# Four buffers for the second layer's weights and stored activations; Hyena's part ahead of the third S5 slice

## The chip, the cores and the metric

The kernel runs on one core of a Trainium2 chip. The metric is the device time of one execution in microseconds (us), the median of several runs. The engines are named as in the profile: PE is TensorE, PEld its weight loads, DVE is VectorE, ACT is ScalarE, POOL is GpSimd, SP is SyncE, which here only issues DMAs. SPq is SP's instruction queue.

## What is computed

One layer of a diffusion backbone for 512 latent tokens of width 1024, with 256 context tokens. First a mixer: half of the projected width goes through an S5 state-space model, the other half through a Hyena operator (gated long convolutions by Fourier transforms). Then PEER, which takes for each token and each of 8 heads the 16 best of 16,384 one-neuron experts:

```python
def block(hb):
    q = (hb @ wq).astype(f32).reshape(hb.shape[0], PEER_HEADS, 2, PEER_DK_HALF)
    ...
    e = (jnp.take_along_axis(i1, ci // PEER_TOPK, axis=-1) * PEER_NKEYS
         + jnp.take_along_axis(i2, ci % PEER_TOPK, axis=-1))
    g = jax.nn.softmax(sc, axis=-1)
    act = jax.nn.gelu(jnp.einsum('chkd,cd->chk', jnp.take(u_tab, e, axis=0), hb).astype(f32))
    return jnp.einsum('chk,chkd->cd', (g * act).astype(hb.dtype), jnp.take(v_tab, e, axis=0))
```

All of it is float32. The tables `u_tab` (the experts' first layer) and `v_tab` (their second layer) hold 16,384 rows of 1024 each, 64 MB a table.

## The kernel before

The program is one stream of instructions that a scheduler orders for each engine before it runs; every engine then works through its own list in order. A tile comes from a pool with a fixed number of buffers (`bufs`); an instruction that writes a tile waits until the readers of the tile that held the buffer before are done.

**The mixer** (up to about 480 us). A loop over eight S5 slices (`s_` from 0 to 7) calls `states` and `from_states`; `added(s_ + 1)` prepares the next slice. Ahead of slice `HYAT` it calls `hyena()`, which projects Hyena's half of the width, runs its transforms and multiplies its half of the output projection (`wout_half(1)`). After the last slice PE transposes the S5 result (`pyt`), and the gated linear unit and `wout_half(0)` follow.

**PEER for the first 128 tokens** takes a gather: `gathered(s)` reads for each of 128 experts places one row of both tables per token with an indirect DMA from POOL into `uvr` (1 MB, three buffers), and DVE makes the dot product (`junk`, L1430) and adds the weighted second half to `accg` (L1438). The 128 gathers are spread over the rest of the program, some 0.6 of one in each pass of the loop below while its index is under 88, 1.5 after that.

**PEER for the other 384 tokens** is dense. `first(i)` multiplies the block of 128 experts `i` of the first layer with the tokens and keeps the activation; 88 blocks (`NRUN`) are made ahead and stored in DRAM as `GA[i]`. The gates come from one-hot products (`gates`, L1558) and are stored in DRAM as `GD`.

**The last loop** (about 1060 to 1820 us) runs over the 128 blocks. Each pass is `second(i, ga)`: SP loads the block's second-layer weights `vr` (L1592, 512 KB), every fourth pass a tile of gates `gc` (L1595, 768 KB), and while `i` is under 88 the stored activation `gal` (L1602, 192 KB). ACT and DVE split `vr` into a high and a low part, `vh` (L1598) and `vl` (L1599); DVE multiplies activation and gate (`gw`, L1604), ACT and DVE split that (`wwh` L1607, `wwl` L1608); PE adds 18 products to six accumulators `pacc`. From pass 87 on `first` makes the remaining 40 blocks between the passes; the scheduler pulls some of these ahead.

The buffers in question are those of `mp`, whose default is two: `vr` has `NVR = 2`, `gal` and `yf` (the residual at the end, L1650) two, `gc` two, `vh`, `vl`, `wwh` and `wwl` three each. SP issues all these loads in one list, in order. So the load of `vr` for pass `i` waits at the head of that list until `vl` of pass `i - 2` is made.

```python
vr = mp.tile([P, D], F32, tag="vr", name=f"vr{i}", bufs=NVR)
nc.sync.dma_start(vr, I["uv"][i * P:(i + 1) * P, D:2 * D])
...
A.activation(vh, vr, AF.Copy)
(V if QUIET or i >= P - VLV else GP).tensor_tensor(vl, vr, vh.bitcast(F32), ALU.subtract)
```

Of the kernel before, what the change touches and what calls it, by code (L numbers as in the profile page):

```python
# [9 lines left out]
F32 = mybir.dt.float32  # L10
F32R = mybir.dt.float32r
# [3 lines left out]
AF = mybir.ActivationFunctionType  # L15
ALU = mybir.AluOpType
AX = mybir.AxisListType

P = 128
D = 1024  # L20
# [65 lines left out]
ND = L - NG  # L86
# [9 lines left out]
GH = 2.0  # L96
NOO = 3
S5M = 1
HYAT = 4
GCN = 4  # L100
FQ = 1
MERGE = 1
RECTS = ((0, 1, 16), (1, 1, 8), (2, 2, 5), (4, 4, 3), (8, 8, 1))
NCAND = 54 if MERGE else 50
NVR = 2
NVH = 3
VLV = 2
AHEAD = 2
# [119 lines left out]
def build(tc, I, out, dbg=None, stop=None):  # L228
# [37 lines left out]
    def ps5(name):  # L266
        return ps.tile([P, 512], F32, tag="p5", name=name, bufs=NP5)
# [4 lines left out]
    def psa(name):  # L272
        return pap.tile([P, 512], F32, tag="pa", name=name)
# [13 lines left out]
    def b2(name, shape, dtype=F32):  # L287
        return cur[0].tile(shape, dtype, tag="b2", name=name, bufs=nb2[0])
# [4 lines left out]
    def sm(name, shape, dtype=F32, bufs=1, tag=None):  # L293
        return cur[0].tile(shape, dtype, tag=tag or name, name=name, bufs=bufs)

    def wblock(src, name, lo_eng=None):
        raw = wp.tile([P, D], F32, tag="wraw", name=name + "r", bufs=NRAW)
        ld(raw, src)
        hi = wp.tile([P, D], F32R, tag="wh", name=name + "h")
        lo = wp.tile([P, D], F32R, tag="wl", name=name + "l")  # L300
        nc.scalar.activation(hi, raw, AF.Copy)
        (lo_eng or (nc.vector if FQ else nc.gpsimd)).tensor_tensor(lo, raw, hi.bitcast(F32), ALU.subtract)
        return hi.rearrange("p (k m) -> p k m", m=P), lo.rearrange("p (k m) -> p k m", m=P)
# [29 lines left out]
    V = nc.vector  # L333
    A = nc.scalar
    GP = nc.gpsimd
    FG = V if FQ else GP
    PE = nc.tensor
# [341 lines left out]
    for part in SEQ.split():  # L679
# [36 lines left out]
        elif part[0] == "S":  # L716
            t0, t1 = ((0, 4), None, (4, 6))[n_]
# [21 lines left out]
        elif part[0] == "P":  # L739
# [5 lines left out]
            if NWARM:  # L745
# [5 lines left out]
                for i in range(NWARM):  # L751
                    mm = PE.matmul(pwarm, warm[:, 0:P], warm, start=True, stop=True)
# [457 lines left out]
    for s_ in range(NSL):  # L1210
        vs = VS
        if s_ + 1 < NSL:
            VS = added(s_ + 1)
        if s_ == HYAT:
            hyena()
# [32 lines left out]
    def g2_(name, shape):  # L1248
        return sg_(name, shape, tag="g2", bufs=NG2)
# [10 lines left out]
    for co in range(4):  # L1260
        wg = sg_(f"wg{co}", [P, 4, P], tag="wg", bufs=2)
        nc.sync.dma_start(wg, I["w_glu"][co].rearrange("p (k m) -> p k m", m=P))
        pg = ps5(f"pg{co}")
# [8 lines left out]
        t = g2_(f"cat5{co}", [P, 512])  # L1272
# [24 lines left out]
    for k in range(8):  # L1297
        t = b2(f"h2t{k}", [P, 512])
# [39 lines left out]
    iotak = sm("iotak", [P, P])  # L1338
# [119 lines left out]
    def gathers(share, after):  # L1458
        due[0] += share
        while due[1] < min(P, due[0]):  # L1460
            gathered(due[1], after)
            due[1] += 1

    for hd in range(8):
# [3 lines left out]
        for e in range(2):  # L1468
            ct = 2 * hd + e
            wh, wl = wblock(I["w_q"][ct], f"wq{ct}", V if FQ or QUIET and ct >= 2 else GP)  # L1470
            pq = psa(f"pq{ct}")
# [23 lines left out]
    def columns(lt, eid, gt):  # L1495

        ei = sm(f"ei{lt}", [P, 2, P], I32, tag="ei", bufs=2)
        V.tensor_copy(ei[:, 0], eid)
        V.tensor_scalar(ei[:, 1], ei[:, 0], 127, None, ALU.bitwise_and)
        V.tensor_scalar(ei[:, 0], ei[:, 0], 7, None, ALU.logical_shift_right)  # L1500
        ef = sm(f"ef{lt}", [P, 2, P], tag="ef", bufs=2)
        V.tensor_copy(ef, ei)
        ptr = ps.tile([P, 512], F32, tag="psc", name=f"ptr{lt}", bufs=2 if RGATE else 3)[:, 0:3 * P].rearrange("p (e n) -> p e n", e=3)
        PE.transpose(ptr[:, 0], ef[:, 0], ident)
        PE.transpose(ptr[:, 1], ef[:, 1], ident)
        PE.transpose(ptr[:, 2], gt, ident)
        if RGATE:
            t = sm(f"cols{lt}", [P, 2, P], tag="cols", bufs=3)
            A.activation(t, ptr[:, 0:2], AF.Copy)
            g = sm(f"colg{lt}", [P, 2, P], F32R, tag="colg", bufs=3)  # L1510
            A.activation(g[:, 0], ptr[:, 2], AF.Copy)
            V.tensor_tensor(g[:, 1], ptr[:, 2], g[:, 0].bitcast(F32), ALU.subtract)
            return t, g.bitcast(F32)
        t = sm(f"cols{lt}", [P, 5, P], tag="cols", bufs=3)
        A.activation(t[:, 0:3], ptr, AF.Copy)
        A.activation(t[:, 3:5], ptr[:, 0:3:2], AF.Copy, scale=-1.0)
        return t

    def gates_r(b_, cols, c0):
        cols, g = cols  # L1520
        st = sm(f"gst{b_}", [P, P, SG], tag="gst", bufs=2)
        for q in range(SG // 4):
            pg = ps.tile([P, 4, 2, P], F32, tag="pgg", name=f"pgg{b_}_{q}", bufs=2)
            t0 = c0 + 4 * q
            oo = sm(f"oo{b_}_{q}", [P, 4, 2, P], F32R, tag="oo", bufs=NOO)
            os_ = sm(f"os{b_}_{q}", [P, 4, 2, P], F32R, tag="os", bufs=NOO)
            V.tensor_tensor(oo, iotak.unsqueeze(1).unsqueeze(1).broadcast_to((P, 4, 2, P)),
                            cols[:, :, t0:t0 + 4].rearrange("p e t -> p t e").unsqueeze(3).broadcast_to((P, 4, 2, P)), ALU.is_equal)
            for e in range(4):
                for h in range(2):  # L1530
                    A.activation(os_[:, e, h], oo[:, e, 0].bitcast(F32), AF.Copy, scale=g[:, h, t0 + e:t0 + e + 1])
            for e in range(4):
                mm = PE.matmul(pg[:, e].rearrange("p h i -> p (h i)"), oo[:, e, 1], os_[:, e].rearrange("p h i -> p (h i)"), start=True, stop=True)
            groups.append(mm)
            so = st[:, :, 4 * q:4 * q + 4]
            A.activation(so, pg[:, :, 0].rearrange("p t i -> p i t"), AF.Copy)
            last = V.tensor_tensor(so, pg[:, :, 1].rearrange("p t i -> p i t"), so, ALU.add)
            gathers(G_SHARE, last)
            run_ahead(RG)
        nc.scalar.dma_start(GD[b_], st)  # L1540
# [32 lines left out]
    cols = [columns(lt, eids[:, lt], gts[:, lt]) for lt in range(1, 4)]  # L1573
# [8 lines left out]
    mp = ms.enter_context(tc.tile_pool(name="mp", bufs=2))  # L1582
# [6 lines left out]
    def second(i, ga):  # L1589
        nonlocal gc  # L1590
        vr = mp.tile([P, D], F32, tag="vr", name=f"vr{i}", bufs=NVR)
        nc.sync.dma_start(vr, I["uv"][i * P:(i + 1) * P, D:2 * D])  # L1592
        if i % GCN == 0:
            gc = mp.tile([P, ND // SG, GCN, SG], F32, tag="gc", name=f"gc{i}")
            nc.sync.dma_start(gc, GD[:, :, i:i + GCN, :].rearrange("b p i t -> p b i t"))  # L1595
        vh = mp.tile([P, D], F32R, tag="vh", name=f"vh{i}", bufs=NVH)
        vl = mp.tile([P, D], F32R, tag="vl", name=f"vl{i}", bufs=NVH)
        A.activation(vh, vr, AF.Copy)  # L1598
        (V if QUIET or i >= P - VLV else GP).tensor_tensor(vl, vr, vh.bitcast(F32), ALU.subtract)  # L1599
        if ga is None:  # L1600
            ga = mp.tile([P, ND], F32, tag="gal", name=f"gal{i}")
            nc.sync.dma_start(ga, GA[i])  # L1602
        gw = mp.tile([P, ND], F32, tag="gw", name=f"gw{i}")
        V.tensor_tensor(gw.rearrange("p (b t) -> p b t", t=SG), ga.rearrange("p (b t) -> p b t", t=SG), gc[:, :, i % GCN], ALU.mult)  # L1604
        wh = mp.tile([P, ND], F32R, tag="wwh", name=f"wwh{i}", bufs=NVH)
        wl = mp.tile([P, ND], F32R, tag="wwl", name=f"wwl{i}", bufs=NVH)
        A.activation(wh, gw, AF.Copy)  # L1607
        last = V.tensor_tensor(wl, gw, wh.bitcast(F32), ALU.subtract)  # L1608
        held.append((i, wh, wl, vh, vl))
        if i < P - HOLD or i == P - 1:  # L1610
            for t in range(NT):
                ts_ = slice(t * P, (t + 1) * P)
                for e in range(2):
                    es_ = slice(e * 512, (e + 1) * 512)
                    for (n, ah_, al_, bh_, bl_) in held:
                        mm3(pacc[t][e], (ah_[:, ts_], al_[:, ts_]), (bh_[:, es_], bl_[:, es_]), n == 0, n == P - 1)
            held.clear()
        return last
# [25 lines left out]
    def residual(t):  # L1644
        xr = mp.tile([P, D], F32, tag="xf", name=f"xf{t}", bufs=4)
        nc.sync.dma_start(xr, X1R[t * P:(t + 1) * P])
        y = mp.tile([P, D], F32, tag="yf", name=f"yf{t}")
        ssq = mp.tile([P, 4], F32, tag="ssq", name=f"ssq{t}", bufs=4)
        for e in range(2):
            V.tensor_tensor(y[:, hs[e]], accg[:, hs[e]] if t == 0 else pacc[t - 1][e], gx2[:, hs[e]], ALU.mult)  # L1650
            (GP if t in T_ADD else V).tensor_tensor(xr[:, hs[e]], y[:, hs[e]], xr[:, hs[e]], ALU.add)
            A.activation(junk[:, hs[e]], xr[:, hs[e]], AF.Square, accum_out=ssq[:, e:e + 1])
        ends.append((xr, ssq))
# [44 lines left out]
```

## Time and profile before

| | |
|---|---|
| Time, median of 3 runs | 1841.48 us (1838.68 to 1842.52) |
| The profiled execution | 1842.49 us |
| Its span, first to last instruction | 1840.7 us |
| Busy: PE, DVE, ACT, POOL | 1692.0, 1492.1, 821.4, 157.6 us |
| Mean granted clock of TensorE | 0.968 |

The page cuts the span into 40 slices of 46 us; a digit is the busy share in tenths. The DMA line is the mean busy share of the core's 16 DMA engines, the line under it what they moved. Windows give the same as numbers for any stretch. Lists of waits say which engine sat idle, for whom, how long in total and how often. Matmuls are pipelined: the busy time of PE counts each with its whole length, while the next one starts earlier, so the distance between starts is the price of one.

### The profile page before, as it was taken

How to read it: one execution, taken by the hardware profiler on the slowest of the kernel's cores; microseconds unless marked ns; L12 is line 12 of the kernel's file. 1: busy time of each engine (PE TensorE's matmuls, PEld its weight loads, DVE VectorE, ACT ScalarE, POOL GpSimd, SP SyncE). 2: the span in 40 equal slices, each digit the busy share in tenths (PEclk: the TensorE clock that was granted, in tenths of full speed). 3: DMA queues.
4: the chain of work that ended last, by engine and by line, in shares of the span. 5: the costliest groups of instructions: out<-in, count | busy, mean ns of one | idle time of the engine just before them, and what ended most of it. 6: DMA issues, size and time to landing. Idle time of an engine off the chain costs nothing.

```text
span 1840.7 us, 24953 instructions
## 1 busy us (share of the span) xinstructions
PE 1692.0 (92%) x8729; PEld 1420.7 (77%) x8731; DVE 1492.1 (81%) x3039; ACT 821.4 (45%) x1616; POOL 157.6 (9%) x158
## 2 busy tenths in 40 slices
PE   5799998879999999999999898989898898999997
PEld 2477654447799999989999886767676777999996
DVE  8866999967689988899999766777787777888886
ACT  3444453134533332348988633343333343444444
POOL 0000000000000000001101101111111112121211
PEclk9899998989899999999999998999999999999998
DMA  9436452322444444466898998999989888999981
GB/s 373 146 99 205 160 173 53 75 71 84 126 151 148 146 148 135 145 233 251 325 335 320 341 350 296 311 331 315 331 311 336 302 279 328 360 329 341 342 312 58
DMA packets 170228, 436.13 MB, mean 237 GB/s; under 512 B 17139, under 2 KB 102004, under 8 KB 150902
## 3 DMA queue, kind: packets, MB, share of 16 engines
q1 hardware_dynamic: 128854, 251.28, 40.6%
q0 software_dynamic: 18432, 134.23, 20.2%
q10 hardware_dynamic: 22816, 49.03, 7.3%
q8 instruction: 69, 1.13, 0.2%
q14 instruction: 57, 0.47, 0.1%
HBM read 381.52 MB, written 52.92 MB: 236 GB/s over the span
## 4 chain that ended last, share of the span: by engine, by line
PE 47%; DVE 13%; DMA 13%; ACT 2%; issue 2%; DVEq 0%; ACTq 0%; SPq 0%
DMA vr<-in_uv_dram 11%; PE pa L308 7%; PE pa L306 6%; PE pa L307 6%; PE pacc L307 5%; PE pacc L306 5%; PE pgg L1558 5%; PE pacc L308 5%; DVE vl L1599 2%; PE pq L308 2%; PE pq L306 2%; PE pq L307 2%; ACT vh L1598 2%; DVE idx L1351 1%; DVE rs L1349 1%
## 5 line engine op out<-in xcount | busy, mean ns | idle before, releaser
L307 PE MATMUL pacc<-vl,wwh 128*128 128x512 f32 x768 | 305.8, 399 | 4.7 <-DVE vl L1599 4.7
L308 PE MATMUL pacc<-vh,wwl 128*128 128x512 f32 x768 | 298.0, 397 | 0.0
L306 PE MATMUL pacc<-vh,wwh 128*128 128x512 f32 x768 | 237.1, 402 | 42.8 <-ACT vh L1598 42.7
L1429 POOL DMA_INDIRECT uvr<-in_uv_dram,gidx x128 | 145.2, 1134 | 1148.1 <-DVE accg L1438 810.5
L1599 DVE TENSOR_TENSOR vl<-vr,vh 128x1024 fp32r<-128x1024 f32 x128 | 156.1, 1222 | 94.8 <-ACT vh L1598 94.6
L306 PEld LDWEIGHTS pacc<-vh,wwh 128*128 128x128 f32 x768 | 144.7, 192 | 83.2 <-ACT vh L1598 55.2
L1598 ACT ACTIVATE vh<-vr 128x1024 fp32r<-128x1024 f32 x128 | 135.0, 1057 | 162.3 <-DMA vr<-in_uv_dram 126.5
L307 PEld LDWEIGHTS pacc<-vl,wwh 128*128 128x128 f32 x768 | 148.0, 193 | 38.1 <-DVE vl L1599 7.4
L308 PEld LDWEIGHTS pacc<-vh,wwl 128*128 128x128 f32 x768 | 147.6, 192 | 31.1
L1438 DVE SCALAR_TENSOR_TENSOR accg<-uvr,wgt,accg 128x1024 f32<-128x1024 f32 x128 | 163.7, 1279 | 4.0 <-ACT wgt L1435 1.2
L1430 DVE SCALAR_TENSOR_TENSOR junk<-uvr,hrow 128x1024 f32<-128x1024 f32 x128 | 155.9, 1218 | 2.2 <-DMA uvr<-in_uv_dram,gidx 2.2
L1607 ACT ACTIVATE wwh<-gw 128x384 fp32r<-128x384 f32 x128 | 66.5, 520 | 131.7 <-PE pacc L307 92.3
L1558 PE MATMUL pgg<-o,o 128*128 128x128 f32 x768 | 95.3, 278 | 4.3 <-ACT o L1554 4.3
L1558 PEld LDWEIGHTS pgg<-o,o 128*128 128x128 f32 x768 | 94.3, 195 | 4.5 <-ACT o L1554 4.5
L1608 DVE TENSOR_TENSOR wwl<-gw,wwh 128x384 fp32r<-128x384 f32 x128 | 70.8, 553 | 32.8 <-ACT wwh L1607 32.7
L1549 DVE TENSOR_TENSOR o<-iotak,cols 128x512 f32<-128x512 f32 x96 | 65.9, 686 | 10.3 <-PE pgg L1558 10.3
L1556 DVE TENSOR_SCALAR o<-iotak,cols 128x128 f32<-128x128 f32 x240 | 70.2, 343 | 0.0
L1433 ACT ACTIVATE wgt<-dots 128x1 f32<-128x1 f32 x128 | 25.4, 199 | 87.4 <-DVE junk L1430 87.1
L1554 ACT ACTIVATE o<-o,cols 128x128 f32<-128x128 f32 x144 | 63.6, 493 | 0.2
L1368 ACT ACTIVATE ga<-pa 128x384 f32<-128x384 f32 x128 | 60.4, 472 | 2.7 <-PE pa L308 2.7
L1560 ACT ACTIVATE gst<-pgg 128x512 f32<-128x512 f32 x96 | 56.7, 591 | 2.5 <-PE pgg L1558 2.2
L1604 DVE TENSOR_TENSOR gw<-gal,gc 128x384 f32<-128x384 f32 x88 | 48.4, 553 | 9.1 <-DMA gal<-GA 8.6
(1812 smaller groups left out, 4141.4 us busy)
## 6 DMA issues: line engine op xcount, KB each, us to landing
vr<-in_uv_dram SPq DMA_DIRECT2D x128, 512.0 KB
GD<-gst ACTq DMA_DIRECT2D x12, 2048.0 KB
gc<-GD SPq DMA_DIRECT2D x32, 768.0 KB
GA<-ga ACTq DMA_DIRECT2D x88, 192.0 KB
gal<-GA SPq DMA_DIRECT2D x88, 192.0 KB
wb<-in_w_ada_dram SPq DMA_DIRECT2D x32, 512.0 KB
wa<-in_w_ada_dram SPq DMA_DIRECT2D x8, 1024.0 KB
KD<-kk SPq DMA_DIRECT2D x16, 256.0 KB
```

The costliest lines, as they stand in the source:

```text
L306: nc.tensor.matmul(o, a[0], b[0], start=start, stop=False)
L307: nc.tensor.matmul(o, a[0], b[1], start=False, stop=False)
L308: nc.tensor.matmul(o, a[1], b[0], start=False, stop=stop_)
L1429: GP.indirect_dma_start(out=uvr, out_offset=None, in_=I["uv"], in_offset=bass.IndirectOffsetOnAxis(ap=gidx[:, s:s + 1], axis=0))
L1430: ins = V.scalar_tensor_tensor(junk, uvr[:, 0:D], 1.0, hrow, ALU.mult, ALU.mult, accum_out=dots[:, s:s + 1])
L1438: V.scalar_tensor_tensor(accg, uvr[:, D:2 * D], wgt[:, s:s + 1], accg, ALU.mult, ALU.add)
L1556: last = V.tensor_scalar(o1[:, e], iotak, cols[:, 0, t:t + 1], cols[:, 2, t:t + 1], ALU.is_equal, ALU.mult)
L1558: mm = PE.matmul(pg[:, e, :], o2[:, e], o1[:, e], start=True, stop=True)
L1598: A.activation(vh, vr, AF.Copy)
L1599: (V if QUIET or i >= P - VLV else GP).tensor_tensor(vl, vr, vh.bitcast(F32), ALU.subtract)
L1607: A.activation(wh, gw, AF.Copy)
L1608: last = V.tensor_tensor(wl, gw, wh.bitcast(F32), ALU.subtract)
```

## The change

`NVR` goes from 2 to 4, so `vr` has four buffers. `gal` gets four as well (`NGAL`). The residual's `yf`, two buffers of its own before, now shares those of `vr`. `HYAT` goes from 4 to 2, so `hyena()` stands ahead of the third slice in the source, and the scheduler orders the mixer anew. The diff also rewrites `gates_r` and its branch of `columns`; `RGATE` is 0 in both kernels, so neither is in the program, and every engine gets the same set of instructions in both.

```diff
-HYAT = 4
+HYAT = 2
 GCN = 4
+NGAL = 4
...
-NVR = 2
+NVR = 4
...
         if ga is None:
-            ga = mp.tile([P, ND], F32, tag="gal", name=f"gal{i}")
+            ga = mp.tile([P, ND], F32, tag="gal", name=f"gal{i}", bufs=NGAL)
             nc.sync.dma_start(ga, GA[i])
...
-        y = mp.tile([P, D], F32, tag="yf", name=f"yf{t}")
+        y = mp.tile([P, D], F32, tag="vr", name=f"yf{t}", bufs=NVR)
```

SP's list in the middle of the last loop, around the tile of gates for passes 52 to 55, before (in `vr44_11615` 44 is the pass, the rest a running number):

```order
L1592 DMA vr44_11615<-in_uv_dram 128x1024
L1592 DMA vr45_11649<-in_uv_dram 128x1024
L1602 DMA gal48_11765<-GA_3935 128x384
L1602 DMA gal49_11803<-GA_3935 128x384
L1595 DMA gc52_11907<-GD_7124 128x12x128
L1592 DMA vr46_11687<-in_uv_dram 128x1024
L1602 DMA gal50_11835<-GA_3935 128x384
L1592 DMA vr47_11725<-in_uv_dram 128x1024
```

The same place after:

```order
L1600 DMA vr47_11725<-in_uv_dram 128x1024
L1610 DMA gal50_11835<-GA_3935 128x384
L1610 DMA gal51_11873<-GA_3935 128x384
L1603 DMA gc52_11907<-GD_7124 128x12x128
L1600 DMA vr48_11757<-in_uv_dram 128x1024
L1610 DMA gal52_11913<-GA_3935 128x384
L1600 DMA vr49_11797<-in_uv_dram 128x1024
L1610 DMA gal53_11945<-GA_3935 128x384
```

Against the same tile of gates the loads of `vr` and `gal` stand two passes earlier.

DVE's list at the end of the mixer, before (H7 to Ci7 and ct belong to the last S5 slice; spt, sp, yy, x2t, catz and rzl to Hyena; YC1 is the S5 result that `pyt` waits for):

```order
L585 TENSOR_TENSOR ru07_3363<-ru07_3363,ru17_3364 128x256 x2
L585 TENSOR_TENSOR Cr7_3372<-ct17_3374,ct27_3375 128x512
L1166 TENSOR_TENSOR sp13_2717<-spt130_2725,spt131_2726 128x512
L1167 TENSOR_TENSOR sp13_2717<-spt132_2727,spt133_2728 128x512
L585 TENSOR_TENSOR ct17_3374<-PC1_871,cre_94 128x512
L585 TENSOR_TENSOR ct27_3375<-PC0_870,cre_94 128x512
L585 TENSOR_TENSOR Ci7_3373<-ct17_3374,ct27_3375 128x512
L1041 TENSOR_TENSOR YC1_1325<-YC1_1325,pk10_3392 128x8x64
```

The same place after:

```order
L586 TENSOR_TENSOR ru07_3363<-ru07_3363,ru17_3364 128x256 x2
L1193 TENSOR_TENSOR yy0_2511<-eo0_2509 128x256
L1194 TENSOR_TENSOR yy0_2511<-eo0_2509 128x256
L586 TENSOR_TENSOR Cr7_3372<-ct17_3374,ct27_3375 128x512
L1195 TENSOR_TENSOR x2t_1674<-x2t_1674,yy0_2511 128x512
L586 TENSOR_TENSOR ct17_3374<-PC1_871,cre_94 128x512
L586 TENSOR_TENSOR ct27_3375<-PC0_870,cre_94 128x512
L1199 TENSOR_SCALAR catz0_2515<-x2t_1674,small_91 128x512
L586 TENSOR_TENSOR Ci7_3373<-ct17_3374,ct27_3375 128x512
L480 TENSOR_TENSOR rzl0_2524<-zsq0_2521,rzh0_2523 128x512
L1042 TENSOR_TENSOR YC1_1325<-YC1_1325,pk10_3392 128x8x64
```

The work on Hyena's first output block now stands between the last steps of the last slice, and the step from `sp13` stands ahead of them.

## Rows read from the trace of the kernel before

**Rows 1.** Page, the span in 40 slices of 46 us: PE, DMA share, GB/s.
```profile
PE   5799998879999999999999898989898898999997
DMA  9436452322444444466898998999989888999981
GB/s 373 146 99 205 160 173 53 75 71 84 126 151 148 146 148 135 145 233 251 325 335 320 341 350 296 311 331 315 331 311 336 302 279 328 360 329 341 342 312 58
```

**Rows 2.** Windows of the last loop: stretch, busy us (instructions) by engine, clock, DMA.
```profile
1062.00:1155.00 93.00, 85.98 (x377) 73.02 (x377) 61.65 (x84) 33.72 (x59) 10.01 (x9) 0.92 0.93 321
1155.00:1504.00 349.00, 314.45 (x1322) 250.27 (x1321) 258.37 (x346) 130.94 (x234) 42.26 (x42) 0.98 0.92 318
1504.00:1560.00 56.00, 50.00 (x223) 42.32 (x222) 46.11 (x58) 22.80 (x45) 14.98 (x11) 0.94 0.86 310
1560.00:1820.00 260.00, 260.00 (x1320) 237.15 (x1319) 209.32 (x262) 115.74 (x220) 47.45 (x41) 1.00 0.86 307
```

**Rows 3.** The same windows, instructions on the accumulators pacc alone (PE, PEld, DVE).
```profile
1062.00:1155.00 93.00, 63.66 (x247) 49.17 (x248) 0.00 (x0) 0.92 0.93 321
1155.00:1504.00 349.00, 312.36 (x1309) 247.88 (x1307) 0.00 (x0) 0.98 0.92 318
1504.00:1560.00 56.00, 39.86 (x158) 30.86 (x156) 0.00 (x0) 0.94 0.86 310
1560.00:1820.00 260.00, 131.95 (x556) 103.97 (x557) 0.00 (x0) 1.00 0.86 307
```

**Rows 4.** Waits of 1155 to 1504: total us, times, longest.
```profile
ACT vh L1598 <- DMA vr<-in_uv_dram: 88.1, 52, 5.5
DVE vl L1599 <- ACT vh L1598: 65.2, 38, 6.4
PE pacc L306 <- ACT vh L1598: 33.2, 24, 4.8
```

**Rows 5.** Waits of SP's own queue, same stretch.
```profile
SPq L1592 <- DVE vl L1599: 115.3, 63, 3.8
SPq L1602 <- DVE gw L1604: 111.0, 54, 4.8
```

**Rows 6.** Chain that ended last, same stretch by line; then pieces: start us, us.
```profile
by line: DMA vr<-in_uv_dram 53.3%; DVE vl L1599 8.2%; ACT vh L1598 7.2%; PE pacc L307 7.1%; PE pacc L306 7.1%; PE pacc L308 6.4%; issue 5.7%; DMA gal<-GA 1.5%; DVE junk L1430 1.5%; DVE gw L1604 1.4%; ACT wwh L1607 0.9%; DVE wwl L1608 0.9%; 
...
1300.89 6.57 DMA vr<-in_uv_dram
...
1307.48 1.07 ACT vh L1598
```

**Rows 7.** DMA from 1062 to 1504: packets; the gathers' queue (share of 16 engines).
```profile
DMA packets 71296, 140.94 MB, mean 319 GB/s; under 512 B 4174, under 2 KB 52302, under 8 KB 64744
...
q0 software_dynamic: 7344, 53.48, 33.0%
```

**Rows 8.** Timeline, first products of two passes that follow without a pause.
```profile
1279.83 1.52 PE L306 MATMUL pacc<-vh,wwh 128*128 128x512 f32 x6
...
1283.91 1.52 PE L306 MATMUL pacc<-vh,wwh 128*128 128x512 f32 x6
```

**Rows 9.** Timeline: the issue of one gather and the first use of its data.
```profile
1282.64 1.01 POOL L1429 DMA_INDIRECT uvr<-in_uv_dram,gidx  x1 [5.93 <-DVE accg L1438]
...
1298.50 1.22 DVE L1430 SCALAR_TENSOR_TENSOR junk<-uvr,hrow 128x1024 f32<-128x1024 f32 x1
```

**Rows 10.** Gathers from 1090 to 1820: issue to landing.
```profile
DMA to landing us min/median/max: 5.5/8.2/11.0
```

**Rows 11.** Windows at the mixer's end, columns as in rows 2.
```profile
322.00:368.00 46.00, 36.94 (x174) 20.34 (x175) 46.00 (x80) 7.49 (x17) 0.10 (x1) 0.93 0.32 75
368.00:414.00 46.00, 32.70 (x156) 22.71 (x155) 30.26 (x49) 18.05 (x33) 0.00 (x0) 0.89 0.23 70
```

**Rows 12.** DVE timeline at the last slice; in brackets idle us before, and for whom.
```profile
377.67 0.69 DVE L1041 TENSOR_TENSOR YC<-YC,pk 128x512 f32<-128x512 f32 x1 [1.47 <-PE pk L1038]
...
400.75 0.69 DVE L1055 TENSOR_TENSOR wout12l<-wout12r,wout12h 128x512 fp32r<-128x512 f32 x1 [0.68 <-ACT wout12h L1054]
```

More of the change, by code (lines that the diff above doesn't have):

```diff
@@ L1507, in columns @@
         if RGATE:
[L1508 to L1513, printed above, removed]
+            t = sm(f"cols{lt}", [P, P], tag="cols", bufs=3)
+            A.activation(t, ptr[:, 1], AF.Copy)
+            gh_ = sm(f"colg{lt}", [P, P], F32R, tag="colg", bufs=3)
+            A.activation(gh_, ptr[:, 2], AF.Copy)
+            V.tensor_tensor(ptr[:, 2], ptr[:, 2], gh_.bitcast(F32), ALU.subtract)
+            return t, gh_.bitcast(F32), ptr
         t = sm(f"cols{lt}", [P, 5, P], tag="cols", bufs=3)
@@ L1519, in gates_r, with per_token @@
     def gates_r(b_, cols, c0):
-        cols, g = cols
+        i2, gh_, ptr = cols
         st = sm(f"gst{b_}", [P, P, SG], tag="gst", bufs=2)
+        def per_token(x, t0):
+            return x[:, t0:t0 + 4].unsqueeze(2).broadcast_to((P, 4, P))
         for q in range(SG // 4):
@@ L1524, in gates_r @@
             t0 = c0 + 4 * q
-            oo = sm(f"oo{b_}_{q}", [P, 4, 2, P], F32R, tag="oo", bufs=NOO)
+            o2 = sm(f"o2_{b_}_{q}", [P, 4, P], F32R, tag="o2", bufs=NOO)
+            o1 = sm(f"o1_{b_}_{q}", [P, 4, P], tag="o1", bufs=NOO)
             os_ = sm(f"os{b_}_{q}", [P, 4, 2, P], F32R, tag="os", bufs=NOO)
-            V.tensor_tensor(oo, iotak.unsqueeze(1).unsqueeze(1).broadcast_to((P, 4, 2, P)),
-                            cols[:, :, t0:t0 + 4].rearrange("p e t -> p t e").unsqueeze(3).broadcast_to((P, 4, 2, P)), ALU.is_equal)
+            keys_ = iotak.unsqueeze(1).broadcast_to((P, 4, P))
+            GP.tensor_tensor(o2, keys_, per_token(i2, t0), ALU.is_equal)
+            V.tensor_tensor(o1, keys_, per_token(ptr[:, 0], t0), ALU.is_equal)
+            V.tensor_tensor(os_[:, :, 1], o1, per_token(ptr[:, 2], t0), ALU.mult)
             for e in range(4):
-                for h in range(2):
-                    A.activation(os_[:, e, h], oo[:, e, 0].bitcast(F32), AF.Copy, scale=g[:, h, t0 + e:t0 + e + 1])
+                A.activation(os_[:, e, 0], o1[:, e], AF.Copy, scale=gh_[:, t0 + e:t0 + e + 1])
             for e in range(4):
-                mm = PE.matmul(pg[:, e].rearrange("p h i -> p (h i)"), oo[:, e, 1], os_[:, e].rearrange("p h i -> p (h i)"), start=True, stop=True)
+                mm = PE.matmul(pg[:, e].rearrange("p h i -> p (h i)"), o2[:, e], os_[:, e].rearrange("p h i -> p (h i)"), start=True, stop=True)
             groups.append(mm)
```

## The prediction

> **What bounds the kernel now.** First the page's slices [rows 1]: from the 20th slice on the DMA engines are nearly always busy, and PE, at 9 tenths before, falls to 8 every other slice or so between the 23rd and the 34th. That is the last loop up to pass 87. The windows give it numbers [rows 2]: from 1560 on PE is busy for 260.00 of 260 us, with the loads of both tables beside it, so this part is bound by PE. From 1155 to 1504 PE has 314.45 of 349 us, DVE 258.37, ACT 130.94, and the DMA engines are 0.92 busy.
>
> Then the waits of that stretch [rows 4]: ACT waits 88.1 us in 52 places for `vr`, DVE 65.2 us for `vh`, and PE for `vh`. One chain, seen at three engines. SP's own queue tells why `vr` is late [rows 5]: it waits 63 times for `vl`, the last reader of the buffer that `vr` goes into. The chain that ended last says it once more: 53.3% of the stretch is `vr` on its way [rows 6]. One turn of it: issued at 1300.89 as soon as `vl` freed the buffer, used at 1307.48, 6.57 us later.
>
> How much room is there? PE's busy time hides it, since products overlap. From one pass's first product to the next one's is 4.08 us when nothing waits [rows 8], for 18 products, 0.227 us each. In 1155 to 1504 stand 1309 products on `pacc` [rows 3], 72.7 passes: 4.80 us a pass. A product of `first` is shorter: in 1560 to 1820 PE is full, so (260 - 556 x 0.227) / 764 = 0.175 us [rows 2, 3].
>
> **The change part by part.** It was profiled at 1842.5 us, 1.0 over the median; I make the sum on the profile and take it from the median.
>
> *Four buffers for* `vr`, from 1062 to 1504 (442 us). SP's list after the change puts the load two passes earlier against the other loads, and the buffer it waits for was freed two passes earlier. So a load has nearly four passes (some 16 us) instead of two, for a transfer that took 6.57 us; the wait on `vl` is gone as a cause. What is late next? Three floors.
>
> PE: 247 + 1309 products on `pacc` at 0.227 and 130 + 13 others at 0.175 [rows 2, 3] make 353 + 25 = 378 us. This would give back 64 us and no more.
>
> DMA by busy share: 0.92 to 0.93 now [rows 2]. The same transfers with the engines never idle take 442 x 0.92 = 407 us: 35 us back.
>
> DMA by bytes: 140.94 MB go through in this stretch [rows 7], and no work is taken out. The fullest slice with gathers and loads together moved 360 GB/s [rows 1], so 392 us: 50 us back. At the 350 GB/s of the 24th slice, where PE stayed at 9 tenths, it is 403 us.
>
> So DMA binds before PE does. I take 404 us (349 GB/s), **38 us back**: near the floor by busy share, since that is measured on just these transfers, and a little better, because where two queues hold packets on one engine the share counts both. For the range: 15 us (share only to 0.95) to 50.
>
> The Trainium skill speaks to this ("DMA: Bandwidth & Descriptors", Specifications): it puts what one core can get from HBM at about 358 GB/s. By that this stretch takes at least 394 us, 48 us back, and the PE floor can't be reached. The trace has the page's first slice at 373 GB/s [rows 1], so it is no hard limit here; but with both queues no slice is above 360, which agrees.
>
> *The first passes after it*, 1504 to 1560: PE is busy 50.00 of 56 us [rows 2]; by count 158 x 0.227 + 65 x 0.175 = 47 us, so up to 9 us are there. The rate of gathers goes from 0.6 to 1.5 a pass here, which deeper buffers don't change: **3 us**, between 0 and 9. From 1560 on PE is full: nothing.
>
> *Four buffers for* `gal`: SP waits 111.0 us in this place [rows 5], but in this stretch no engine is listed as waiting for `gal`. What it does is let SP reach the next `vr` sooner; it is part of the 38 us and nothing by itself.
>
> *`yf` in the buffers of* `vr`: the four last `vr` are read by `vl` before the residual begins, so no new wait: 0.
>
> *`hyena()` ahead of the third slice*: the same instructions in another order. DVE is full to 368 [rows 11], so a change of order gains nothing there. After that it is busy 30.26 of 46 us. Between 376 and 401 it idles nine times, 0.6 to 1.7 us each, for PE and ACT (the first and the last: [rows 12]), some 9 us in all. The new order puts Hyena's first output block among the last steps of the last slice, which fills the first of these pauses, but puts five short operations ahead of `YC1`, which `pyt` waits for. Bounds: 9 us back if all pauses close, 6 lost if two or three more of that length open. I take **2 us back**, since two pauses are filled and a part of it is paid by `YC1`. PE is the bound from here to pass 0, so the difference is not swallowed later.
>
> Sum: 38 + 3 + 2 = 43 us; 1841.5 - 43 = **1798 us**.
>
> **The rivals.**
>
> *DMA is the bound already.* For it: 0.92 busy. Then more loads in flight only wait longer beside each other, and the share creeps to 0.95: 442 x (1 - 0.92 / 0.95) = 14 us, time 1827; with nothing at all back, 1841. Against it: 53.3% of the chain is `vr` alone, with SP standing at `vl` before each load, and the wait of ACT ends some 6 us after the issue, most of which is queue time that could begin earlier.
>
> *It doesn't do what it says: SP's list holds the loads up elsewhere.* `vr48` stands behind `gc52` and `gal51`, each of which waits for a `gw`; if those come free only shortly before `vl`, the load gets three passes and not four. For it: SP already waits 111.0 us for `gw` [rows 5]. Against it: none of these waits is longer than 4.8 us, little over a pass. Half of the 38 us: 1841.5 - 19 - 3 = 1820.
>
> *PE is the bound after all*: 64 + 2 us back, 1775. It needs 140.94 MB in 378 us, 373 GB/s, more than any slice with both queues moved.
>
> *Slower: the gathers starve.* Place: `junk` on DVE, ahead of `vl` in the same list. A gather is issued when its buffer is free and used 15.86 us later [rows 9]; it lands after 8.2 us, at most 11.0 [rows 10], so DVE hardly waits. With shorter passes the lead falls to 15.86 x 404 / 442 = 14.5 us, and SP's queue, always filled, takes more of the engines. 53.48 MB at 1.05 MB [rows 7] are 51 gathers; each us over the lead costs 51 us. From 15.4 us on, the 43 us are gone; at 16 us it is 1841.5 - 43 + 76 = 1875. Against it: landing would have to double.
>
> The Trainium skill has a rule on it ("DMA: Bandwidth & Descriptors", Queues, rings and completion order): an engine goes round robin between the queues that have work. By that a gather keeps half of the engines; half of 360 GB/s moves 1.05 MB in 5.8 us, and the lead holds. No run yet shows it with SP's queue always full; it is why this rival gets so little.
>
> **How the numbers follow.** Forecast 0.62; DMA bound already 0.17; held up elsewhere 0.10; PE bound 0.07; gathers 0.04. The range: low, the DMA floor by bytes with 50 + 9 + 6 = 65 us, 1776; high, 15 us, 1826. It holds the forecast, the delayed case and about half of the first rival: 8 in 10. Within 0.2% (3.7 us, about what a measurement of this kernel can tell from no change) lies the poorest end of the first rival, 0.04; slower is the starved gather and a bad order of the mixer without the gain, 0.04; faster 0.92.
>
> **What would show it.** Right: in the last loop up to pass 87 some 4.4 us a pass; SP's wait for `vl` and ACT's for `vr` down to a fraction of 115.3 and 88.1 us; DMA share near 1 and 345 to 360 GB/s; the part after 1560 as long as before; gathers landing later, but under 14 us. Wrong: the same GB/s with longer loads (first rival); SP standing at `gw` before each `vr` (second); 4.1 us a pass with DMA under 0.95 (third); DVE idle before `junk` (fourth). If the mixer ends more than 9 us earlier or 6 us later, the order counts for more than I give it.

## The result, and the profile after

The changed kernel takes **1781.09 us** (median of 4 runs, 1779.70 to 1784.46); the kernel before, on the same chip, 1841.59 us. The ratio is 0.9677, 95% interval 0.9659 to 0.9695: 60 us gained, where 43 were forecast. The profiled execution took 1782.07 us, its span 1780.3 us.

Where they lie, by landmarks in the two traces (us from the start of the span; the load of `vr` 0 is SP's issue, `vh` 87 and 97 are ACT's copies of these passes):

| | before | after | gained in between |
|---|---|---|---|
| load of `vr` 0 | 1059.9 | 1057.6 | 2.3 |
| `vh` of pass 87 | 1503.3 | 1446.3 | 54.7 |
| `vh` of pass 97 | 1559.2 | 1498.8 | 3.4 |
| last product on `pacc` | 1828.6 | 1768.2 | 0.0 |

So nearly all of it is in the stretch of the first 88 passes. From here on "the stretch" is the time from the load of `vr` 0 to `vh` 87: 443.4 us before, 388.7 after. From pass 14 to 87 a pass takes 4.29 us instead of 4.77.

Windows of the changed kernel, in the order of [rows 2]: the stretch, busy us (instructions) of PE, PEld, DVE, ACT and POOL, granted clock, DMA share, GB/s. The four stretches answer to the four of [rows 2], moved by what was gained ahead of them.

```profile
1059.00:1133.00 74.00, 73.95 (x338) 63.44 (x339) 56.87 (x81) 30.91 (x54) 12.21 (x8) 0.97 1.04 377
1133.00:1447.00 314.00, 303.88 (x1336) 248.76 (x1335) 260.26 (x347) 129.30 (x235) 47.86 (x43) 1.00 1.01 360
1447.00:1499.00 52.00, 52.00 (x247) 45.11 (x246) 43.93 (x56) 21.96 (x44) 11.35 (x9) 1.00 0.91 322
1499.00:1760.00 261.00, 261.00 (x1324) 238.00 (x1323) 213.54 (x268) 117.18 (x224) 54.44 (x43) 1.00 0.86 309
```

PE is full or close to it in all four, the DMA engines are at 1.01 to 1.04 in the first two, and the last row is that of [rows 2] again. The page's slices say the same, beside [rows 1]: from the 25th on PE no longer falls to 8 every other slice, and five slices in a row move 356 to 387 GB/s.

```profile
PE   5799998789899999998999989999999999999997
...
DMA  9436453122444444446989899999999998999981
GB/s 372 155 98 209 156 170 91 51 75 71 124 156 139 141 147 151 145 147 246 330 319 333 322 321 387 385 356 378 363 353 358 357 339 320 342 327 349 335 311 71
```

The waits of the second stretch (total us, times, longest):

```profile
ACT wwh L1615 <- PE pacc L308: 131.1, 70, 4.1
...
PE pacc L307 <- ACT vh L1606: 8.4, 7, 1.3
DVE vl L1607 <- ACT vh L1606: 4.8, 6, 1.2
```

Of [rows 4] the first row is gone: ACT no longer waits for `vr`. DVE's 65.2 us for `vh` are 4.8, PE's 33.2 are 8.4. What ACT waits for most now is PE, to give a buffer of `wwh` back. PE's granted clock was 0.92 and 0.98 in the first two stretches of [rows 2] and is 0.97 and 1.00 now: before, 49 products of these passes started 0.40 to 0.45 us after the one ahead of them, where 0.227 is usual; after the change none did. What these slow products cost before isn't shown, since PE was not the bound then (`l_before` below).

SP's own queue, though, looks as it did [rows 5]:

```profile
SPq L1610 <- DVE gw L1612: 124.9, 54, 4.3
SPq L1600 <- DVE vl L1607: 83.4, 61, 7.4
```

SP still stands at `vl` and `gw` before most loads, since it runs ahead until every buffer is taken. These waits now cost nothing: in passes 14 to 87 a load of `vr` is used 9.2 to 18.4 us after its issue (median 13.1), before 3.5 to 11.1 (median 6.3). The chain of the same stretch, against [rows 6], where `vr` on its way had 53.3%:

```profile
by line: PE pacc L308 29.9%; PE pacc L309 29.1%; PE pacc L307 28.6%; issue 2.6%; DVE junk L1431 1.5%; DMA gal<-GA 1.5%; ACT vh L1606 1.3%; DVE vl L1607 1.2%; ACT wwh L1615 0.9%; PE pa L309 0.7%; PE pa L307 0.7%; PE pa L308 0.7%; DVE gw L161
```

Last the DMA view of both first stretches together, beside [rows 7]: the same 141 MB in 388 us, and the share of the gathers' queue and of SP's (q1) add up to more than 1.

```profile
DMA packets 71373, 140.91 MB, mean 363 GB/s; under 512 B 4174, under 2 KB 52302, under 8 KB 64905
...
q1 hardware_dynamic: 64105, 87.81, 66.0%
q0 software_dynamic: 7244, 52.79, 35.2%
```

### The profile page after: what moved, and what is told of

It reads as the page before. It is cut to its first block, busy times and chain, and to the rows that moved or that the text cites. A ratio compares the mean times of both kernels' runs of the same rounds, so it can differ in the third digit from the quotient of the medians.

```text
span 1780.3 us, 24942 instructions
## 1 busy us (share of the span) xinstructions
PE 1670.0 (94%) x8731; PEld 1410.6 (79%) x8731; DVE 1491.0 (84%) x3039; ACT 817.9 (46%) x1616; POOL 169.5 (10%) x158
## 4 chain that ended last, share of the span: by engine, by line
PE 63%; DVE 12%; issue 1%; ACT 1%; DMA 1%; ACTq 0%; DVEq 0%
PE pacc L308 9%; PE pacc L309 9%; PE pacc L307 9%; PE pa L309 7%; PE pa L307 7%; PE pa L308 7%; PE pgg L1566 5%; PE pq L309 2%; PE pq L307 2%; PE pq L308 2%; DVE idx L1352 1%; DVE rs L1350 1%; PE pg L1266 1%; DVE idx L1348 1%; PE po L307 1%
## 5 line engine op out<-in xcount | busy, mean ns | idle before, releaser
L308 PE MATMUL pacc<-vl,wwh 128*128 128x512 f32 x768 | 299.6, 391 | 1.8 <-DVE vl L1607 1.8
L1430 POOL DMA_INDIRECT uvr<-in_uv_dram,gidx x128 | 157.1, 1228 | 1090.6 <-DVE accg L1439 764.6
L308 PEld LDWEIGHTS pacc<-vl,wwh 128*128 128x128 f32 x768 | 144.1, 188 | 33.6 <-DVE vl L1607 3.6
```

The source lines that it names most:

```text
L308: nc.tensor.matmul(o, a[0], b[1], start=False, stop=False)
L1430: GP.indirect_dma_start(out=uvr, out_offset=None, in_=I["uv"], in_offset=bass.IndirectOffsetOnAxis(ap=gidx[:, s:s + 1], axis=0))
```

## The experiments

Ratios are to the kernel before, measured beside each run, so they can be set beside 0.9677 of the change. Gains in us are differences of medians; by the ratios they come out some 3 us otherwise at most. In the last loop the scheduler ordered the lists of ACT, DVE and SP anew in each of these kernels, so that a few us can also come from the order. Theory 1 was that `vr` had been issued too late for its landing time and that PE is the bound now. The rivals: DMA is the bound now, SP's list or `gal` held the loads up, or the order of the mixer gave more than it seems.

### The parts of the change alone

The buffers without the order (`p_bufs`, against the changed kernel):

```diff
-HYAT = 2
+HYAT = 4
```

> All of the change except HYAT, which stays 4. Theory 1 (late loads of vr were the loss, and the mixer's order gave 2.2 us): the loop as in the changed kernel, pass 0 begins 2 us later, 1783 us. Rival A (the new order of the mixer counts for more than its 2.2 us at pass 0, because the loop's instructions are ordered anew as well): over 1788 us.

Measured: 1786.42 us, ratio 0.9693 (0.9663 to 0.9723). The stretch takes 393.5 us. The buffers make nearly the whole gain; the order's share, 0.0016 or 3 us, is within the intervals.

The order without the buffers (`p_hyat2`, against the kernel before):

```diff
-HYAT = 4
+HYAT = 2
```

> HYAT = 2 alone, all buffers as before. Theory 1: the first transpose of the S5 result and the first pass of the last loop come 1 to 3 us earlier, the passes stay at 4.8 us, 1839 us. Rival A: the loop changes too, under 1834 us.

Measured: 1837.69 us, ratio 0.9959 (0.9939 to 0.9980): 7.6 us gained against the 1845.26 us measured beside it, more than the 1 to 3 of theory 1, and as much as rival A asked for (under 1834 us, with 1841.5 before). Where it is gained is seen only roughly, since the one profiled run took 1832.05 us, 5.6 less than the median. In that run it isn't the mixer: `pq`, the first product after it, starts at 479.3 us (479.5 before). By pass 14 the run is 7.4 us ahead. With another order of the mixer the lists of DVE, ACT and SP differ around the first passes of the loop too, on SP in some ten places, and are the same after that. That this makes the 7.6 us is not shown: from the load of `vr` 0 to `vh` 14 `p_hyat2` takes 87.2 us and the kernel before 94.9, but `l_before` below, with `HYAT` = 4 and fewer products, 87.0 as well.

How far the mixer can be told apart at all shows in two kernels whose lists on PE are the same up to the last loop, `p_gal3` and `p_vr3` below. Their first products of `pq` (duration ns min/median/max, first and last start up to 486 us):

```profile
L307 PE MATMUL pq<-h2h,wq0h x6: 387/395/796, 476.8 to 485.2; 128*128 128x512 f32 x6
```

```profile
L307 PE MATMUL pq<-h2h,wq0h x3: 398/632/768, 481.5 to 485.6; 128*128 128x512 f32 x3
```

The same order starts it at 476.8 and at 481.5 us. Over all profiled runs it starts at 479.9 us on average with `HYAT` = 2 (8 kernels) and at 480.0 with 4 (6 kernels). The 2.3 us of the table above are within this scatter.

Four buffers for `vr` alone (`p_vr4`):

```diff
-HYAT = 2
+HYAT = 4
...
-NGAL = 4
+NGAL = 2
```

> Four buffers for vr alone (yf shares them, as in the change, since the memory does not hold both); gal keeps two, HYAT stays 4. Theory 1: 4.3 us a pass, 1783 us, as with four buffers for gal. Rival B (SP, held at the load of gal until gw frees its buffer, gets to vr only a pass later): half of the gain in the loop, some 1812 us, with ACT waiting again for vr.

Measured: 1813.30 us, ratio 0.9831 (0.9802 to 0.9860), about half of the gain: rival B's number, but not by its mechanism. ACT waits for `gw`, not for `vr`; the waits of 1138 to 1475:

```profile
ACT wwh L1615 <- DVE gw L1612: 60.1, 38, 3.4
...
DVE gw L1612 <- DMA gal<-GA: 34.0, 20, 4.0
```

And its chain there, with one of its longest pieces (start us, us):

```profile
by line: DMA gal<-GA 26.3%; PE pacc L307 17.1%; PE pacc L309 16.6%; PE pacc L308 16.2%; issue 4.0%; ACT vh L1606 3.5%; DVE accg L1439 3.2%; DVE vl L1607 3.1%; DVE gw L1612 3.1%; DVE junk L1431 2.0%; DMA gc<-GD 1.9%; ACT wwh L1615 1.6%; DVE 
...
1302.68 11.11 DMA gal<-GA
```

The load of `gal` is issued as `gw` of two passes earlier ends (1302.64) and lands 11.11 us later. Before the change two passes were 9.6 us, and `gal` came just in time (`gw` waited 8.6 us for it in the whole program), hidden by `vr`, which was later still. With `vr` early, two passes would be 8.6 us, and `gal` takes `vr`'s place as the late load.

Four buffers for `gal` alone (`p_gal4`):

```diff
-HYAT = 2
+HYAT = 4
...
-NVR = 4
+NVR = 2
...
-        y = mp.tile([P, D], F32, tag="vr", name=f"yf{t}", bufs=NVR)
+        y = mp.tile([P, D], F32, tag="yf", name=f"yf{t}")
```

> Four buffers for gal alone; vr keeps two and yf its own, HYAT stays 4. Theory 1: the load of vr still waits for vl of two passes before, 4.8 us a pass, 1841 us. Rival B: the wait for gw was part of the lateness, 1820 us.

Measured: 1849.69 us, ratio 1.0030 (1.0008 to 1.0051). Nothing, or a little lost, as theory 1 said. So -32 us for `vr` alone, +4 for `gal` alone, -59 for both (p_bufs): the parts don't add up, because each hides the other.

### Three buffers

`p_vr3` and `p_gal3`, each against the changed kernel:

```diff
-NVR = 4
+NVR = 3
```

> The changed kernel with three buffers for vr instead of four. Theory 1 (what counts is that the load is issued earlier than its landing time before its use): three passes of 4.3 us are 12.8 us, against a landing of some 6 to 11 us, so nearly all of the gain stays, 1781 to 1790 us. Rival (the gain comes with the amount of loads in flight): half of the gain, some 1811 us.

```diff
-NGAL = 4
+NGAL = 3
```

> The changed kernel with three buffers for gal instead of four. Theory 1: with two buffers gal is issued two passes (8.6 us) before its use and lands after 9 to 11 us, with three it is 12.8 us, enough: 1781 to 1785 us. Rival (gal must stand as many passes ahead as vr, since both are in one list): some 1797 us.

Measured: 1787.97 us, ratio 0.9708 (0.9686 to 0.9731), and 1790.08 us, ratio 0.9727 (0.9703 to 0.9751). By the ratios three buffers keep 54 and 50 of the 60 us. It is the lead that counts: with three buffers a load of `vr` is used 3.7 to 12.1 us after its issue (median 8.9), and the pieces shown above took 6.57 and 11.11 us to land. ACT still waits 14.6 us for `vr` in 14 places of the second stretch, at most 2.9.

What the fourth buffer is worth is less clear. By the ratios it is 6 us for `vr`, where the intervals overlap, and 9 for `gal`. In the profiled runs the stretch takes 389.8 us with three for `vr`, 1.1 more than with four (the loop began 4.8 us later), and 392.6 with three for `gal`, 3.9 more. There DVE waits only 0.8 us for `gal` from 1133 to 1447, so that late loads are not shown to be the cause.

### What binds after the change

The load of `gal` doubled (`x2_after`):

```diff
-            ga = mp.tile([P, ND], F32, tag="gal", name=f"gal{i}", bufs=NGAL)
-            nc.sync.dma_start(ga, GA[i])
+            ga = mp.tile([P, 2, ND], F32, tag="gal", name=f"gal{i}", bufs=NGAL)
+            nc.sync.dma_start(ga, GA[i].unsqueeze(1).broadcast_to((P, 2, ND)))
+            ga = ga[:, 0]
```

> The changed kernel, with the load of gal doubled: the second half of its 384 KB is not used. 17.3 MB more in 88 passes. Theory 1 (PE is the bound now, the DMA engines have room up to the 385 GB/s that slices reach): 158.2 MB need 411 us where the passes 0 to 87 now take 388, so 0 to 25 us more, 1781 to 1806 us. Theory 2 (DMA is the bound now, at the 363 GB/s of this stretch): 48 us more, 1829 us.

Measured: 1831.05 us, ratio 0.9937 (0.9916 to 0.9959): 50 us more, theory 2's number. The stretch takes 438.1 us, with the share of the DMA engines at 1.01:

```profile
1062.60:1500.70 438.10, 396.02 (x1689) 324.11 (x1689) 320.67 (x433) 161.27 (x292) 61.04 (x51) 0.96 1.01 364
```

That the loads alone make the 50 us is not shown. At the 381 GB/s of `l_after` below, the 159.6 MB of this stretch would take 419 us, 30 more than in the changed kernel. The chain of 1133 to 1450 hardly names a load:

```profile
by line: PE pacc L307 28.1%; PE pacc L308 27.2%; PE pacc L309 25.7%; DMA vr<-in_uv_dram 5.6%; ACT vh L1606 3.2%; issue 3.2%; DVE junk L1431 2.6%; ACT wwh L1616 1.9%; DVE vl L1607 1.1%; ACT wgt L1434 0.4%; DVE gw L1613 0.3%; DVE wwl L1617 0.
```

PE waits 33.7 us there for `vh`, while ACT waits for `vr` only once, 3.5 us; and PE's granted clock is 0.95, where it was 1.00. What holds up ACT's `vh` is open; the order of its list may have a part in it.

A third of the loop's products left out (`l_after`):

```diff
-                        mm3(pacc[t][e], (ah_[:, ts_], al_[:, ts_]), (bh_[:, es_], bl_[:, es_]), n == 0, n == P - 1)
+                        if n < NRUN and n > 0:
+                            nc.tensor.matmul(pacc[t][e], ah_[:, ts_], bh_[:, es_], start=False, stop=False)
+                            if e == 0:
...
```

> The changed kernel with a third of the last loop's products left out in passes 1 to 87 (six of 18: those with the low parts, for the second half of the width), so that PE needs about 2.9 us a pass; all loads and all work of DVE and ACT stay. Theory 1 (PE is the bound now): the passes get shorter until DMA or DVE binds, 140.9 MB at 385 GB/s are 366 us for 388, so 1759 us. Theory 2 (DMA is the bound now): 0 to 3 us less, 1778 us.

Measured: 1761.15 us, ratio 0.9550 (0.9523 to 0.9578): 20 us less, theory 1's number. The stretch takes 371.6 us for 141.5 MB, and PE is busy in 298.8 of them:

```profile
1062.00:1433.60 371.60, 298.81 (x1184) 237.55 (x1185) 313.88 (x428) 160.26 (x289) 68.26 (x51) 0.91 1.04 381
```

This is the most that the DMA engines need for these bytes, not the least: in the chain of 1133 to 1450 PE's products still have 33.5%, the loads of `vr` and `gal` 20.2%.

Three of four loads of `gal` left out (`y_after`):

```diff
-            ga = mp.tile([P, ND], F32, tag="gal", name=f"gal{i}", bufs=NGAL)
-            nc.sync.dma_start(ga, GA[i])
+            if i % 4 == 0:
+                kept = mp.tile([P, ND], F32, tag="gal", name=f"gal{i}", bufs=NGAL)
+                nc.sync.dma_start(kept, GA[i])
+            ga = kept
...
```

> The changed kernel with the load of gal left out in three passes of four (the tile loaded in the fourth is used for all four), so 12.7 MB less in passes 0 to 87; everything else stays. Theory 1 (PE is the bound after the change): 0 to 5 us less, 1776 to 1781 us. Theory 2 (DMA is the bound after the change, at 363 GB/s): 35 us less, 1746 us.

Measured: 1771.00 us, ratio 0.9625 (0.9584 to 0.9667), 10 us less: twice theory 1's most and under a third of theory 2's. The stretch takes 371.0 us, and here PE is what is full:

```profile
1057.50:1428.50 371.00, 368.58 (x1637) 307.67 (x1638) 311.37 (x426) 158.84 (x286) 53.62 (x51) 0.99 0.97 343
```

The three together answer neither theory but both. With a third of PE's products gone the DMA engines get through the stretch in 371.6 us. With loads of `gal` gone PE gets through in 371.0. Its stretch has 31 products of `first` fewer than that of the changed kernel; that one's 1536 products on `pacc` and 136 others need 372 us at the prediction's 0.227 and 0.175. The changed kernel takes 388.7: two floors at nearly the same height, and 17 us over them (PE busy 378.4 of the 388.7). That now and then one waits for the other would explain the 17 us, but no run shows it. Taking work from either side gave time (20 and 10 us), and loads added cost it; adding work to PE was not tried. Why the doubled load ran at 364 GB/s and not at the 381 of `l_after` is open: it moved 82,942 packets (189 a us), `l_after` 71,384 (192 a us), so a limit by packets would fit, and so would ACT's late `vh`, but no run tried either.

The same products left out of the kernel before (`l_before`, same edit as in `l_after`):

> The kernel before with the same third of the last loop's products left out as in l_after (the low parts for the second half of the width, passes 1 to 87). Theory 1 (before the change each vr was issued too late, and PE was not the bound): 0 to 10 us less than before, 1832 to 1842 us. Rival (PE and the loads took turns, so that both bound): as much as in l_after or more, under 1822 us.

Measured: 1845.55 us, ratio 1.0018 (0.9990 to 1.0046). Before the change a third less work on PE gave nothing. PE, busy in 320.7 of the 458.6 us, was not the bound, nor were the DMA engines, at a share of 0.89 and 308 GB/s:

```profile
1060.10:1518.70 458.60, 320.73 (x1197) 241.35 (x1198) 321.25 (x433) 162.39 (x293) 59.48 (x52) 0.89 0.89 308
```

The stretch even takes 15 us more than before, with PE's granted clock at 0.89, and the passes behind it 12.5 less; why is open.

### A version that might beat both

The scale of the residual made before the stored blocks of the first layer (`v_early`, the lines moved ahead, with tiles of another pool):

```diff
+    gx2 = rt("gx2", [P, D])
+    gfin = rt("gfin", [P, D])
+    nc.sync.dma_start(gfin, I["g_final"].broadcast_to((P, D)))
...
-    gx2 = mp.tile([P, D], F32, tag="gx2", name="gx2", bufs=1)
-    gfin = mp.tile([P, D], F32, tag="gfin", name="gfin", bufs=1)
-    nc.sync.dma_start(gfin, I["g_final"].broadcast_to((P, D)))
...
```

> The changed kernel, with the scale of the residual (gx2, gfin and the small products pgx) made before the first layer's stored blocks instead of just ahead of the last loop. There PE idles 8.9 us in both kernels, since gx2 takes memory that the last store of the gates still reads. Theory 1 (PE is the bound throughout): these 9 us are gained in full, 1772 us. Rival (the loads of the first passes bind there): pass 0 starts earlier and waits, 0 to 3 us, 1779 us.

> As v_early, with hyena() where it was before (HYAT = 4). Theory 1 (the order of the mixer is worth the 2.2 us seen at pass 0): 2 us more than v_early. Rival (it is worth the 7 us that HYAT = 2 alone showed): 7 us more.

Measured: 1783.59 us, ratio 0.9670 (0.9629 to 0.9710), and with `HYAT` = 4 1784.33 us, ratio 0.9690 (0.9654 to 0.9726). Neither beats the change, nor does one `HYAT` beat the other by more than the interval. PE's pause is filled: between the last product of the gates and the first on `pacc` the longest distance between two starts is 1.5 us, against 9.1 in the changed kernel. But pass 0 comes only 3.3 us earlier after the last product of the gates. A part of the rest went into 30 more products of `first` that now stand ahead of it, an estimated 5 us at 0.175. And the chain from 1049 to 1075 has the last store of the gates (`GD`) and the load of `gal` behind it, near to what the rival said:

```profile
by line: DMA GD<-gst 48.4%; DMA gal<-GA 26.9%; PE pgg L1566 6.1%; DVE u91l L303 4.7%; issue 3.7%; DVE vl L1617 3.6%; DVE gw L1622 2.5%; ACT gst L1568 2.3%; SPq L1613 2.0%; SPq L1610 1.4%; DVE wwl L1626 0.3%; DVEq L1622 0.1%
```

## Why the prediction was right, and where its sum was off

**The cause** was named rightly: `vr` was issued too late, and one chain showed at three engines. `l_before` shows that PE wasn't the bound, `p_vr4` and `p_vr3` that the lead counts. Nearly all of the stretch's gain comes from the buffers (50 of 55 us by `p_bufs`).

**The term for the stretch** was mis-sized: 38 us forecast, 54.7 measured between the landmarks (388.7 us; the forecast's 404 were for a window 1.4 us shorter). The step that was off is "So DMA binds before PE does", and in it two floors. The prediction's bound for this term, 50 us, was exceeded too. That its range (1776 to 1826 us) held is partly luck: the 9 + 6 us that it added for other stages, of which 3.4 and 2.3 came, made up for it. In that sum the 6 is the mixer's loss; its gain was bounded by 9.

- The floor by busy share, 407 us, was none. It took 0.92 of the engines' time as work that must be done. The share counts the packets of two queues on one engine twice where they overlap, which the prediction said in passing and then corrected by 3 us only. After the change the share is 1.01 to 1.04, in `l_after` 1.04: the same packets fit into 371.6 us. Nor is time x share a fixed sum: 0.92 x 443.4 = 408 us before, 1.04 x 371.6 = 386 in `l_after`.
- The floor by bytes, 392 us, used 360 GB/s, the fullest slice seen with both queues moving. But the engines waited for work in that trace, and slices of 46 us average over these waits. Cut into 40 slices of 10 us from 1090 to 1500, the same trace shows up to 400 GB/s:

```profile
GB/s 338 344 259 352 273 276 304 294 309 318 354 336 292 339 355 313 331 329 258 400 304 317 299 370 272 315 351 298 359 333 321 308 337 271 268 278 394 335 305 332
```

After the change five slices of the page in a row read 387, 385, 356, 378 and 363, and `l_after` holds 381 over the whole stretch.

The Trainium skill ("DMA: Bandwidth & Descriptors", Specifications) puts what one core can get from HBM at about 358 GB/s; from this the prediction had its estimate of 394 us at least. Another page of the Trainium skill ("Perfetto Trace Analysis", Roofline) says that this is the share of a core while both cores of a pair are at work, and that one alone can pull up to some 120% of it. The prediction drew on the first alone. The 363 GB/s of the changed kernel and the 381 of `l_after` agree with the second.

The floor of PE, 378 us, was close: 371.0 in `y_after`. The rival "PE is the bound after all" with 1775 us got 0.07 and came nearer than the forecast, in its number and in the chain, which is PE's by 87.6%, though it asked for "DMA under 0.95". The truth lies between the two: both are nearly full.

**The other rivals.** "DMA is the bound already" expected the same GB/s with longer loads; the stretch went from 319 to 363 GB/s. "SP's list holds the loads up elsewhere" did not come with four buffers for both, as the leads of 9.2 to 18.4 us show.

**The boundary**, 3 us: 3.4. **From pass 97 on**, nothing: 0.0 of 269.4 us.

**The order of the mixer**, 2 us: the pair of profiles shows 2.3 ahead of the loop, but the scatter of one and the same order is 4.7 us, and the averages differ by 0.1. The term is not confirmed. Alone, the order gave 7.6 us, in the one profiled run within the loop's first passes, which the prediction hadn't looked at; with the buffers it gave at most a few.

**`gal`**: "nothing by itself" held (ratio 1.0030 alone). "What it does is let SP reach the next `vr` sooner" did not. Without it 27 of the 59 us are lost, because `gal` itself is late as soon as a pass is shorter than half its landing time. The row for it was there: SP waited 54 times for `gw` to free a buffer before it issued `gal` [rows 5], so that this load had some two passes, 9.6 us, and no more. The prediction laid that wait to SP's account alone and gave `gal` no landing time of its own.

**`yf`** in the buffers of `vr`: nothing, from the last product on `pacc` to the end of the span it is 12.1 us in both.

**The signs.** "Some 4.4 us a pass": 4.29. "DMA share near 1": 1.01 to 1.04; "345 to 360 GB/s": 363. ACT's wait for `vr` down to a fraction: gone. SP's wait for `vl` down to a fraction: wrong as a sign, 83.4 us of 314 against 115.3 of 349; a queue that runs ahead waits for buffers all the same.

**The slower rival**, starved gathers, did not come. Issue to landing of the gathers from 1090 to 1760, against [rows 10]:

```profile
DMA to landing us min/median/max: 5.5/8.7/10.3
```

The median is 0.5 us later, the longest 0.7 us earlier, and DVE's 2.2 us of waiting for a gather in the whole program are no longer listed. The Trainium skill's rule ("DMA: Bandwidth & Descriptors", Queues, rings and completion order) that an engine goes round robin between the queues with work agrees with this: with SP's queue at 66.0% of the engines' time a gather lands almost as before. The estimate of 5.8 us that the prediction made from it was low; the medians are 8.2 and 8.7.

## What to carry to other kernels

Compare each load's lead (issue to first use) with its landing time, in passes of the length that is hoped for, and deepen together all loads that fall short: one late load hides the next, so buffers that are worth nothing alone can be worth half of the gain. A wait in the issuing queue says nothing by itself; whether anyone waits for the data does. Floors of a resource are read from a stretch in which it was never left without work, and a busy share over two queues is not one of them.

## What was not expected of the hardware

The mean busy share of the 16 DMA engines goes over 1 where two queues hold packets (1.04 in `l_after`), and 381 GB/s were held for 371.6 us by one core, with 53 MB of gathers among 141.5 MB. With a third of the products gone PE pauses more, and its granted clock falls from 0.99 to 0.91 over the stretch (0.89 in `l_before`), so the products left in `l_after` ran partly at the lower of its two levels (1.2 and 2.4 GHz).
